# A hybrid encoder trunk: Fourier weight tiles by output half, q swaps right behind the eviction, exponentials scaled on GpSimd

## The chip, the cores and the metric

The kernel runs on one core of one Trainium2 chip. The metric is the device time of one execution in microseconds. Before the change the median of three runs is 2400.9 us (2396.56 to 2402.89).

## What is computed

Two layers over 272 tokens (16 meta tokens and 256 real ones), model width 2048, all in float32. Per layer, cut to what matters here:

```
h = rmsnorm(x);  [q | k | v | f | ga | gf] = h @ w_in
attention: 8 query heads on 2 key heads of 128; q and k are normalised
           per head and rotated (rope on four quarters of 32 channels)
           p = softmax(q k^T / sqrt(128));  o = p v
fourier:   Re(2-D DFT over positions and the 128 channels of a group) of f
a = o @ w_attn_br;  s = fourier @ w_four
x = x + (sigmoid(ga) * a + sigmoid(gf) * s) @ w_out
x = x + w_down( silu(dwconv3(rmsnorm(x) @ w_up_gate)) * (rmsnorm(x) @ w_up_val) )
```

## The kernel before, in words

Activations lie transposed in SBUF, channels on partitions. Each weight passes through once as a stream of chunks of 512 KB: 128 partitions by 4 blocks of 256 columns. SyncE's queue loads a chunk into one of seven `raw` buffers (`load_raw`). For precision each float32 operand is split in two parts: ScalarE casts the high part `wh` (line 300), VectorE subtracts for the low part `wl` (line 303), each with three buffers. A matmul group then takes three products per block, high by high, high by low and low by high (lines 372 to 374).

The order of the work is the order in which the program emits it. `order` lists all weight groups. `advance(upto)` issues loads up to seven chunks past `upto` and puts the splits up to `upto` on a list; `pump()` emits one of that list after every second triple of matmuls, and `pump(i)` emits all up to chunk i. Side work (norm statistics, rotation, attention, the DFT) sits in generators on a `shadow` list; `step()` advances one of them at each of the same points, and a yielded number is how many steps that generator rests. A scheduler then lays the instructions into the queues of the engines. Two things bind it: instructions under `keep_in_program_order` stay where they were emitted, and inside `manual_schedule(engines=...)` so does all work of the named engines.

Three places are touched.

**The Fourier branch, `four_group`.** Each of the eight groups per layer computes s for 256 outputs in two halves m of 128. Its 8 row blocks of w_four come as two chunks. A chunk holds half the input rows of both output halves, so each half m runs through both chunks (loop j, then c, then the even and odd part e): sixteen matmuls per half on lines 407 (high weights on high and low data at once) and 408 (low weights), and one matmul for the remaining channels (line 413). `pump(i0 + 1)` emits both chunks' splits ahead of the first matmul. In layer 0 each of these chunks is first folded on VectorE (`fold_w`, line 291: sums and differences of row halves) into the tile `wpm`, which has one buffer; the split reads `wpm`. Layer 1's chunks were folded earlier and stored (`prefold`).

**q.** After each of the four q groups per layer, `head_evac` (lines 910 and 911) reads the product from PSUM: squares into `qps` on ScalarE, the scaled q into `qp` on VectorE. Then the generator `q_stage` is pushed. Its first step issues `swap` (line 924): four DMAs from SyncE's queue that write qp with neighbouring quarters of 32 partitions exchanged into `qs`. Later steps take the statistics (lines 918 to 1029, the power of line 513 on GpSimd) and rotate: `rope` (lines 928 to 933) multiplies qs by the sines and qp by the cosines, adds and splits. The tiles qp, qps and qs share seven buffers (tag "r") with the gates and with layer 1's folding. In layer 1 q group 1 and the folded Fourier projection behind it (`folded_f`, 16 chunks of folded weights `fw`, matmuls of lines 843 to 847) run with VectorE's order written by hand; so the rotation of q0 stands at a fixed place in VectorE's queue, between splits.

**Attention.** Per key head there are nine items of 128 query rows: one of meta tokens and eight of a head and a block. `scores` makes the product into PSUM, its row maximum and the exponentials `pe` with their sum `sm` (line 1078). `normalise` takes the reciprocal `rs` (line 1083) and multiplies pe by it into `pn`, in two VectorE instructions (lines 1086 and 1087; the second writes the 16 meta columns three times). An iteration later `transposed` turns pn on TensorE (line 1095) and splits it into PH and PL (lines 1108, 1109); after another iteration `values` multiplies by v (lines 1118 to 1121). Matmuls of the q and gate groups run between the steps. GpSimd has little to do in this stage; its queue carries the DMAs that add up weights for the last layer (`weight_sums`, lines 558 and 559), each behind a one-column copy `tick` from the newest low part.

Of the kernel before, what the change touches and what calls it, by code (L numbers as in the profile page):

```python
# [13 lines left out]
ALU = mybir.AluOpType  # L14
AX = mybir.AxisListType

P = 128
D = 2048
NM = 16
SEQ = 256  # L20
T = NM + SEQ
# [5 lines left out]
NG = 8  # L27
# [5 lines left out]
CW = 4  # L33
MG = 2
# [43 lines left out]
TH = T // 2 + 2  # L78
# [75 lines left out]
def _rep(ap, n):  # L154
    return ap.unsqueeze(1).to_broadcast([ap.shape[0], n, ap.shape[1]])
# [8 lines left out]
def st2(ap):  # L164
    if len(ap.shape) == 3:
        return ap.rearrange("p r (a b) -> p r a b", b=2)
    return ap.rearrange("p (a b) -> p a b", b=2)
# [11 lines left out]
def encoder_kernel(ctx, tc, xT, params, consts, bmat, cfold, csign, w_fl, w_f64c, w_in, w_abr, w_four, w_f64, w_out, w_up, w_down, w_vn, w_dn, w_dt, out):  # L179
    nc = tc.nc  # L180
# [12 lines left out]
    for l in range(DEPTH):  # L193
# [13 lines left out]
        for half in range(2):  # L207
            for kind, j in BRANCH_ORDER[half]:
                w, off, n = {"ga": (w_in, IN_GA, KT), "gf": (w_in, IN_GF, KT), "s": (w_four, 0, 8), "a": (w_abr, 0, 8)}[kind]
# [25 lines left out]
    t, done = 0, 0  # L235
    for key, chs in order:
        for j, ch in enumerate(chs):
            n = 0
            if key[0] == 1 and key[1] in ("t", "ug", "uv"):
                n = due(t) - done  # L240
# [40 lines left out]
    def pump(upto=None):  # L281
        if upto is None:
            if todo:
                todo.pop(0)[1]()
        while upto is not None and todo and todo[0][0] <= upto:
            todo.pop(0)[1]()
# [101 lines left out]
    def four_group(key, fr, x64, w64, evac):  # L388
        k, chs = order[st["grp"]]
        assert k == key, (k, key)  # L390
        st["grp"] += 1
        i0 = st["next"]
        st["next"] += len(chs)
        advance(i0 + 1 + LOOK)
        pump(i0 + 1)
        ws = [splits.pop(i0 + j) for j in range(2)]
        for m in range(MG):
            sl = slice(m * P, (m + 1) * P)
            ps = [psum.tile([P, 512], F32, tag="mm", name=f"ps_s{m}{e}") for e in range(2)]
            for j in range(2):  # L400
                h, lo = ws[j]
                for c in range(2):
                    kt = 2 * j + c
                    for e in range(2):
                        x = al(fr[:, kt, e])
                        o2 = st2(ps[e][:, :2 * TH].rearrange("p (r n) -> p r n", r=2))
                        nc.tensor.matmul(o2, h[:, 2 * e + c, sl], x, start=kt == 0, stop=False)
                        nc.tensor.matmul(st2(ps[e][:, :TH]), lo[:, 2 * e + c, sl], x[:, 0], start=False, stop=e == 1 and kt == 3)
                    step()
                    pump()  # L410
                if m == 1 and j == 0:
                    advance(i0 + 2 + LOOK)
            nc.tensor.matmul(st2(ps[0][:, :TH]), w64[:, sl], al(x64), start=False, stop=True)
            evac(m, ps)
# [194 lines left out]
    for l in range(DEPTH):  # L609
# [6 lines left out]
        with tc.tile_pool(name=f"mix{l}", bufs=1) as mp:  # L616
# [285 lines left out]
            def head_evac(ps, gcol, name, lo):  # L902
                hp = rt(name)
                sq = rt(name + "s")
                if lo:
                    nc.gpsimd.memset(hp[:, :, 0:lo], 0.0)
                    nc.gpsimd.memset(sq[:, :, 0:lo], 0.0)
                for m in range(MG):
                    x = de(ps[m][:, :T - lo])
                    nc.scalar.activation(hv(sq[:, m, lo:T]), x, AF.Square)  # L910
                    nc.vector.scalar_tensor_tensor(hv(hp[:, m, lo:T]), x, gcol, hv(rstdB[:, lo:T]), op0=ALU.mult, op1=ALU.mult)
                return hp, sq
# [8 lines left out]
            def swap(hp):  # L921
                qs = rt("qs")
                for b in range(4):
                    tc.keep_in_program_order(nc.sync.dma_start(qs[32 * b:32 * b + 32, :, :], hp[32 * (b ^ 1):32 * (b ^ 1) + 32, :, :]))
                return qs
# [82 lines left out]
            for pn in pns:  # L1008
                nc.gpsimd.memset(pn[:, 0:P], 0.0)

            def q_stage(i, qp, qsq):
                kv, j = i // 2, i % 2
                sl = slice(2 * j, 2 * j + 2)
                if j == 0:
                    qvs.append(small.tile([P, 9], F32, tag="qv", name="qv"))
                    qsms.append(small.tile([P, 2, 4, NM], F32, tag="sqm", name="sqm", bufs=2))
                qv, qsm = qvs[kv], qsms[kv]
                qs = swap(qp)
                yield 3
                nc.vector.tensor_copy(qsm[:, :, 2 * j:2 * j + 2, :], qsq[:, :, 0:NM].unsqueeze(1).to_broadcast([P, 2, 2, NM]))  # L1020
                d4 = qv[:, 4 * j:4 * j + 4]
                sums_t(d4, [qsq[:, m, a:b] for m in range(MG) for a, b in BLK[1:]])
                d4 = d4.rearrange("p (m i) -> p m i", m=2)
                nc.vector.tensor_tensor(d4, d4, bc2(tok2[:, 1:3]), op=ALU.mult)
                if j:
                    yield 1
                    sums_t(qv[:, 8:9], [qsm.rearrange("p r h t -> p (r h t)")])
                    nc.vector.tensor_tensor(qv[:, 8:9], qv[:, 8:9], tok2[:, 0:1], op=ALU.mult)
                    nc.vector.tensor_scalar(qv, qv, 1.0 / HD, EPS, op0=ALU.mult, op1=ALU.add)
                    rq = small.tile([P, 9], F32, tag="rq", name="rq")  # L1030
                    pow_half(rq, qv)
                yield 6 - j
                yield from rope(qp, qs, qH[kv][:, sl, :], qL[kv][:, sl, :])
                if j:
                    rqs.append(rq)
                    if kv == 0:
                        push(attend(), 5)
# [9 lines left out]
            def attention(kv, rq):  # L1047
# [33 lines left out]
                def normalise(pe, sm):  # L1081
                    rs = small.tile([P, 1], F32, tag="rs", name="rs")
                    nc.vector.reciprocal(rs, sm)
                    pn = pns[cnt[0] % 3]
                    cnt[0] += 1
                    nc.vector.tensor_scalar(pn[:, P:3 * P], pe[:, NM:T], rs, None, op0=ALU.mult)
                    nc.vector.tensor_scalar(pn[:, 0:96].rearrange("p (a b) -> p a b", b=32)[:, :, 0:NM], _rep(pe[:, 0:NM], 3),
                                            rs, None, op0=ALU.mult)
                    return pn

# [60 lines left out]
            for i in range(4):  # L1151
                if not (last and i == 1):
                    ps = group((l, "q", i), xr(lo), W)
                    qq = head_evac(ps, prm[:, P_QN + l:P_QN + l + 1], "qp", lo)
                if last:
                    if i in (0, 2):
                        until(hold, "vt" if i == 0 else "fold")
                        for t_, n in ((qH, "q1"), (qL, "q2")):
                            t_.append(mp.tile([P, 4, T], F32R, tag=n + "ab"[i // 2], name=n))
                elif i == 0:  # L1160
                    until(hold, "vt")
                    until(hold, "fold")
                    for t_, n in ((qH, "q1"), (qL, "q2")):
                        t = mp.tile([P, NH, T], F32R, tag=n, name=n)
                        t_ += [t[:, 0:4], t[:, 4:8]]
                if last and i == 1:
                    until(hold, "ahead")
                    with tc.manual_schedule(engines={mybir.EngineType.DVE}):
                        ps = group((l, "q", i), xr(lo), W)
                        with tc.manual_schedule(engines={mybir.EngineType.Activation}):  # L1170
                            qq = head_evac(ps, prm[:, P_QN + l:P_QN + l + 1], "qp", lo)
                            folded_f(slots, E)
                    o1_tiles()
                    push(folded_chan(E), 1)
                push(q_stage(i, *qq), 1)
# [327 lines left out]
def _tiles(w):  # L1503
    d, k, m = w.shape
    return np.ascontiguousarray(
        w.reshape(d, k // (CW * P), CW, P, m // (MG * P), MG * P).transpose(0, 4, 1, 3, 2, 5)
    )


def _four(w):  # L1510
    d = w.shape[0]
    wz = np.concatenate([w, np.zeros((d, 1, D), w.dtype)], 1)
    c = np.arange(HC)
    pair = lambda q: [np.concatenate([P * g + c for g in (2 * q, 2 * q + 1)]),
                      np.concatenate([np.where(c == 0, NG * P, P * g + P - c) for g in (2 * q, 2 * q + 1)])]
    rows = np.concatenate([pair(2 * h + q)[k] for h in range(2) for k in range(2) for q in range(2)])
    w64 = np.zeros((d, 64, D), w.dtype)
    w64[:, 0:8] = w64[:, 32:40] = w[:, [P * (2 * i + m) + HC for m in range(2) for i in range(4)]]
    w64 = np.ascontiguousarray(w64.reshape(d, 64, NG, MG * P).transpose(0, 2, 1, 3))
    return _tiles(wz[:, rows]), w64  # L1520


def _fl(w):
# [47 lines left out]
```

## Time and profile before

| | us |
|---|---|
| median of 3 runs | 2400.9 |
| the profiled execution | 2399.24 |
| its span, first to last instruction | 2397.2 |
| TensorE busy | 2367.0 (99%) |
| VectorE busy | 1819.8 (76%) |
| ScalarE busy | 1307.1 (55%) |
| GpSimd busy | 133.4 (6%) |

The span and the busy times come from one profiled execution. Its stages, in us from the span's start:

| stretch | what runs | TensorE busy | VectorE busy |
|---|---|---|---|
| 0 to 85 | layer 0: norm, f, k, v | 80.00 | 64.59 |
| 85 to 470 | layer 0: q, attention, gates, Fourier and attention branches, first half of w_out | 375.94 | 297.49 |
| 470 to 1240 | layer 0: rest of w_out, feed-forward | 770.00 | 523.84 |
| 1240 to 1680 | layer 1: k to the branches, first half of w_out | 430.42 | 336.15 |
| 1680 to 2397 | layer 1: rest of w_out, feed-forward | 710.62 | 597.77 |

How to read the rows below: a row of a group names the line, engine, operation and tensors (out<-in), the count, and after the bar busy time and mean ns of one. A row of the timeline has start and length in us, and in brackets how long the engine sat idle before and what ended that. A row of the waits names who waited for whom: total us, times, longest. A row of stretches gives the length, each engine's busy us with its instructions in brackets, then the granted clock of TensorE as a share, the DMA share and GB/s. PE is TensorE, PEld its weight loads, DVE VectorE, ACT ScalarE, POOL GpSimd, SPq SyncE's queue. Matmuls are pipelined, so one of 272 columns spans 0.28 us though the next starts 0.116 us after it.

### The profile page before, as it was taken

What the parts mean: (1) busy time and instruction counts of PE and PEld (TensorE: products, weight loads), DVE (VectorE), ACT (ScalarE), POOL (GpSimd) and SP (SyncE); (2) the same over time, 40 slices, a digit from 0 to 9 for tenths busy, and PEclk for the clock granted to TensorE, in tenths of its full rate; (3) what the DMA queues carried; (4) which work ended last, traced back from release to release, by engine and by line L of the source; (5) the groups of instructions that cost most, each with busy time, mean ns of one, the idle gap of its engine ahead of it and who ended that gap; (6) DMA issues with size and microseconds to landing.
All of it is one profiled execution on the core that took longest, in us unless ns stands there. A gap on an engine that the chain in (4) does not pass through costs nothing.

```text
span 2397.2 us, 47622 instructions
## 1 busy us (share of the span) xinstructions
PE 2367.0 (99%) x18992; PEld 2305.8 (96%) x18992; DVE 1819.8 (76%) x2889; ACT 1307.1 (55%) x1893; POOL 133.4 (6%) x265
## 2 busy tenths in 40 slices
PE   9999999999999999999999999999999999999999
PEld 8999999999999999999998999999989999999988
DVE  7787867877767556777568887776878889888798
ACT  6555534554444334444455555445676666666565
POOL 0000100100000000000000000000000000000000
PEclk9999999999999999999999999999999999999999
DMA  7556999989999999999875646888889988988887
GB/s 278 173 159 216 289 295 304 297 278 346 313 303 327 315 330 314 316 327 308 264 256 181 190 150 216 264 291 247 290 294 301 323 291 301 305 304 279 260 279 251
DMA packets 171215, 660.69 MB, mean 276 GB/s; under 512 B 19424, under 2 KB 24672, under 8 KB 170096
## 3 DMA queue, kind: packets, MB, share of 16 engines
q1 hardware_dynamic: 152528, 538.07, 64.0%
q0 software_dynamic: 17024, 117.45, 19.4%
q8 instruction: 149, 2.44, 0.4%
q10 hardware_dynamic: 1440, 2.13, 0.3%
q14 instruction: 74, 0.61, 0.1%
HBM read 635.91 MB, written 136.31 MB: 322 GB/s over the span
## 4 chain that ended last, share of the span: by engine, by line
PE 81%; DVE 6%; ACT 2%; DMA 1%; issue 1%; SPq 0%; POOL 0%; ACTq 0%; DVEq 0%; POOLq 0%
PE ps_p L1415 9%; PE ps_ug L374 6%; PE ps_ug L373 6%; PE ps_ug L372 6%; PE ps_uv L368 4%; PE ps_d L374 3%; PE ps_uv L373 3%; PE ps_uv L372 3%; PE ps_d L373 3%; PE ps_uv L374 3%; PE ps_d L372 3%; DVE wl L303 3%; PE ps_o L372 2%; PE ps_o L373 2%; PE ps_o L374 2%; PE ps_uv L369 2%
## 5 line engine op out<-in xcount | busy, mean ns | idle before, releaser
L303 DVE TENSOR_TENSOR wl<-raw,wh 128x1024 fp32r<-128x1024 f32 (+1 forms) x937 | 1127.6, 1217 | 469.8 <-ACT wh L300 458.4
L300 ACT CAST wh<-raw 128x1024 fp32r<-128x1024 f32 (+1 forms) x937 | 964.6, 1040 | 752.1 <-PE ps_ug L373 197.2
L374 PE MATMUL ps_ug<-xHL,wl 128*128 128x272 f32 (+1 forms) x1408 | 390.6, 277 | 0.8 <-DVE wl L303 0.6
L372 PE MATMUL ps_ug<-xHL,wh 128*128 128x272 f32 (+1 forms) x1408 | 390.7, 278 | 0.0
L373 PE MATMUL ps_ug<-xHL,wh 128*128 128x272 f32 (+1 forms) x1408 | 390.0, 277 | 0.0
L373 PEld LDWEIGHTS ps_ug<-xHL,wh 128*128 128x128 f32 x1408 | 267.4, 190 | 2.1
L372 PEld LDWEIGHTS ps_ug<-xHL,wh 128*128 128x128 f32 x1408 | 267.4, 190 | 2.1
L374 PEld LDWEIGHTS ps_ug<-xHL,wl 128*128 128x128 f32 x1408 | 267.5, 190 | 1.6 <-DVE wl L303 1.5
L372 PE MATMUL ps_uv<-xHL,wh 128*128 128x272 f32 x704 | 196.4, 279 | 0.0
L373 PE MATMUL ps_uv<-xHL,wh 128*128 128x272 f32 x704 | 196.4, 279 | 0.0
L374 PE MATMUL ps_uv<-xHL,wl 128*128 128x272 f32 x704 | 196.4, 279 | 0.0
L372 PE MATMUL ps_d<-gHL,wh 128*128 128x272 f32 x704 | 196.4, 279 | 0.0
L373 PE MATMUL ps_d<-gHL,wh 128*128 128x272 f32 x704 | 196.4, 279 | 0.0
L374 PE MATMUL ps_d<-gHL,wl 128*128 128x272 f32 x704 | 196.4, 279 | 0.0
L1415 PE MATMUL ps_p<-wh,opnd 128*128 128x512 f32 x688 | 177.5, 380 | 0.5 <-ACT wh L300 0.5
L368 PE MATMUL ps_uv<-xHL,wh 128*128 128x512 f32 x448 | 150.8, 383 | 0.1
L372 PE MATMUL ps_ga<-xHL,wh 128*128 128x272 f32 (+1 forms) x512 | 144.0, 281 | 0.0
L372 PE MATMUL ps_gf<-xHL,wh 128*128 128x272 f32 (+1 forms) x512 | 143.0, 279 | 0.0
L374 PE MATMUL ps_gf<-xHL,wl 128*128 128x272 f32 (+1 forms) x512 | 141.8, 277 | 0.0
L373 PE MATMUL ps_ga<-xHL,wh 128*128 128x272 f32 (+1 forms) x512 | 141.8, 277 | 0.0
L374 PE MATMUL ps_ga<-xHL,wl 128*128 128x272 f32 (+1 forms) x512 | 141.8, 277 | 0.0
L373 PE MATMUL ps_gf<-xHL,wh 128*128 128x272 f32 (+1 forms) x512 | 141.8, 277 | 0.0
(372 smaller groups left out, 5840.8 us busy)
## 6 DMA issues: line engine op xcount, KB each, us to landing
raw<-in_w_up SPq DMA_DIRECT2D x320, 512.0 KB, 5.6
raw<-in_w_in SPq DMA_DIRECT2D x191, 512.0 KB, 4.5
raw<-in_w_down SPq DMA_DIRECT2D x88, 512.0 KB, 6.8
raw<-ft SPq DMA_DIRECT2D x80, 512.0 KB, 4.8
raw<-in_w_out SPq DMA_DIRECT2D x64, 512.0 KB, 6.5
ft<-in_w_dn POOLq DMA_DIRECT2D x30, 1024.0 KB, 12.1
raw<-in_w_dn SPq DMA_DIRECT2D x60, 512.0 KB, 5.0
raw<-in_w_abr SPq DMA_DIRECT2D x32, 512.0 KB, 5.6
```

The source lines that it names most:

```text
L300: nc.scalar.copy(h[:, a:b], r[:, a:b])
L303: nc.vector.tensor_tensor(lo[:, a:b], r[:, a:b], h[:, a:b].bitcast(F32), op=ALU.subtract)
L368: nc.tensor.matmul(o2, h[:, c, sl], ab, start=kt == 0, stop=False)
L369: nc.tensor.matmul(o, lo[:, c, sl], ab[:, 0], start=False, stop=kt == nk - 1)
L372: nc.tensor.matmul(o, h[:, c, sl], a, start=kt == 0, stop=False)
L373: nc.tensor.matmul(o, h[:, c, sl], b, start=False, stop=False)
L374: nc.tensor.matmul(o, lo[:, c, sl], a, start=False, stop=kt == nk - 1)
L1415: nc.tensor.matmul(st2(ps[h]), x, al(w[:, 512 * h:512 * h + 512]), start=fresh and (s_, q) in BEGIN and first, stop=(s_, q) in END and end ...
```

## The change

Three edits, and the host's layout of one weight:

- `w_four` is laid out anew, so that a chunk holds all input rows of 128 outputs, instead of half the rows of 256. Each half m of a Fourier group takes one chunk whole. The splits of chunk i0 + m are forced just ahead of half m, and the next `advance` comes at the end of half 0 instead of after the first chunk of half 1. The fold adds and subtracts the same halves of a chunk as before.
- `swap` of q is called right behind `head_evac`, ahead of everything of the next group, and its tile is handed to `q_stage`. The swap of k stays where it was.
- The two multiplications of `normalise` are issued on GpSimd.

```
@@ four_group
         advance(i0 + 1 + LOOK)
-        pump(i0 + 1)
-        ws = [splits.pop(i0 + j) for j in range(2)]
         for m in range(MG):
             sl = slice(m * P, (m + 1) * P)
             ps = [psum.tile([P, 512], F32, tag="mm", name=f"ps_s{m}{e}") for e in range(2)]
+            pump(i0 + m)
+            h, lo = (w.rearrange("p c n -> p (c n)").rearrange("p (e k n) -> p e k n", e=2, k=4) for w in splits.pop(i0 + m))
             for j in range(2):
-                h, lo = ws[j]
                 for c in range(2):
                     kt = 2 * j + c
...
-                        nc.tensor.matmul(o2, h[:, 2 * e + c, sl], x, start=kt == 0, stop=False)
-                        nc.tensor.matmul(st2(ps[e][:, :TH]), lo[:, 2 * e + c, sl], x[:, 0], start=False, stop=e == 1 and kt == 3)
+                        nc.tensor.matmul(o2, h[:, e, kt], x, start=kt == 0, stop=False)
+                        nc.tensor.matmul(st2(ps[e][:, :TH]), lo[:, e, kt], x[:, 0], start=False, stop=e == 1 and kt == 3)
                     step()
                     pump()
-                if m == 1 and j == 0:
+                if m == 0 and j == 1:
                     advance(i0 + 2 + LOOK)
@@ q_stage
-            def q_stage(i, qp, qsq):
+            def q_stage(i, qp, qsq, qs):
...
-                qs = swap(qp)
                 yield 3
@@ normalise
-                    nc.vector.tensor_scalar(pn[:, P:3 * P], pe[:, NM:T], rs, None, op0=ALU.mult)
-                    nc.vector.tensor_scalar(pn[:, 0:96].rearrange("p (a b) -> p a b", b=32)[:, :, 0:NM], _rep(pe[:, 0:NM], 3),
+                    nc.gpsimd.tensor_scalar(pn[:, P:3 * P], pe[:, NM:T], rs, None, op0=ALU.mult)
+                    nc.gpsimd.tensor_scalar(pn[:, 0:96].rearrange("p (a b) -> p a b", b=32)[:, :, 0:NM], _rep(pe[:, 0:NM], 3),
                                             rs, None, op0=ALU.mult)
@@ the q groups (both places)
                     qq = head_evac(ps, prm[:, P_QN + l:P_QN + l + 1], "qp", lo)
+                    qq += (swap(qq[0]),)
@@ _four (host)
-    return _tiles(wz[:, rows]), w64
+    t = _tiles(wz[:, rows]).reshape(d, NG, 2, P, 2, 2, MG, P).transpose(0, 1, 6, 3, 4, 2, 5, 7)
+    return np.ascontiguousarray(t).reshape(d, NG, MG, P, CW, MG * P), w64
```

More of the change, by code (lines that the diff above doesn't have):

```diff
@@ L1171, in encoder_kernel @@
                             qq = head_evac(ps, prm[:, P_QN + l:P_QN + l + 1], "qp", lo)
+                            qq += (swap(qq[0]),)
                             folded_f(slots, E)
```

## The prediction

> **What bounds the kernel now.** I read the page's first part, then the waits of the matmul engine, then the stretches in which those waits lie.
>
> ```profile
> span 2397.2 us, 47622 instructions
> ## 1 busy us (share of the span) xinstructions
> PE 2367.0 (99%) x18992; PEld 2305.8 (96%) x18992; DVE 1819.8 (76%) x2889; ACT 1307.1 (55%) x1893; POOL 133.4 (6%) x265
> ```
>
> PE is busy 99% of the span, and the change removes no matmul. Only PE's own holes can be won back: 30.2 us of plain idle time, and what a lower clock or a modelled end hides inside "busy". PE's waits between 120 and 1700 us, longest first (total us, times, longest):
>
> ```profile
> PE ps_s L408 <- DVE wl L303: 4.3, 8, 0.7
> PE ps_f L847 <- DVE wl L303: 3.9, 1, 3.9
> PE ps_pt L1095 <- DVE pn L1086: 2.9, 4, 1.3
> PE ps_pv L1119 <- DVE PL L1109: 2.2, 4, 1.2
> PE ps_pv L1118 <- ACT PH L1108: 2.0, 5, 0.5
> PE ps_s L407 <- ACT wh L300: 2.0, 5, 1.1
> ```
>
> First and last row: the Fourier groups (ps_s) wait for the split of a weight tile, 6.3 us. Second row: one single wait of 3.9 us in the folded projection of layer 1. The other three, 7.1 us, are attention's. Each of these is the place of one edit.
>
> **Edit 1, the Fourier tile.** A group is 34 matmuls on two tiles. Five of layer 0's eight groups, each from its first matmul to the next group's, and last one of layer 1 (the first number after the stretch is its length):
>
> ```profile
> 222.67:228.74 6.07, 4.34 (x34) 3.99 (x34) 0.51 (x2) 0.45 (x2) 1.00 0.33 99
> 245.47:250.71 5.24, 4.34 (x34) 3.98 (x34) 0.50 (x2) 0.44 (x2) 1.00 0.91 222
> 355.73:360.98 5.25, 4.34 (x34) 3.99 (x34) 0.51 (x2) 0.45 (x2) 1.00 0.93 311
> 388.83:393.31 4.48, 4.12 (x34) 3.92 (x34) 0.51 (x2) 0.45 (x2) 1.00 0.65 164
> 453.50:457.99 4.49, 4.13 (x34) 3.93 (x34) 0.51 (x2) 0.45 (x2) 1.00 0.71 276
> 1576.37:1580.22 3.85, 3.85 (x34) 3.85 (x34) 0.50 (x2) 0.45 (x2) 1.00 0.60 193
> ```
>
> The same 34 matmuls take 3.85 us when nothing is late. Layer 0 loses 2.22 us in its first group, about 1.4 in each of four (the second and third rows are the first and last of them), about 0.63 in each of three (the fourth and fifth rows): 2.22 + 4 x 1.4 + 3 x 0.63 = 9.7 us. Inside another of the four, which began at 289.35, and VectorE's (DVE) load beside it:
>
> ```profile
> 290.58 0.62 PE L407 MATMUL ps_s<-fr,wh 128*128 128x276 f32 x3 [0.20 <-ACT wh L300]
> 291.84 0.44 PE L408 MATMUL ps_s<-fr,wl 128*128 128x138 f32 x2 [0.64 <-DVE wl L303]
> ```
> ```profile
> 289.40:294.50 5.10, 4.26 (x35) 3.91 (x35) 5.01 (x11) 3.91 (x7) 0.00 (x0) 1.00 0.83 339
> ```
>
> The second tile is asked for a quarter of the way in, and both its halves are late: in layer 0 a tile is folded before it is split, through one wpm buffer, so two tiles come one after the other. After the change output half m=0 needs tile 0 alone, and tile 1 is asked for after half the group instead of a quarter, 3.85/4 = 0.96 us later. Each group keeps what exceeds that: 1.26, four times 0.44, three times nothing, 3.0 in all; 6.7 us are won. Matmuls, shapes, loads and splits stay as many. Tile 0's buffers come free at half instead of three quarters and the next `advance` moves up as far, at no cost, since both only let loads and splits start sooner. But VectorE works 5.01 of 5.10 us there, so PE, arriving earlier at the next group, will sometimes find the next tile unfinished. I take a fifth back, 1.3 us (bounds: nothing, and 0.44 in each of eight groups, 3.5). **Edit 1: -5.4 us** (-3.2 to -6.7).
>
> **Edit 2, the q swaps.** The second wait, with the tensors of VectorE and SyncE (SPq) that lead to it:
>
> ```profile
> 1293.55 0.29 PE L846 MATMUL ps_f<-hA,w64s 128*16 128x138 f32 x2
> 1297.73 0.48 PE L847 MATMUL ps_f<-hA,wl 128*128 128x138 f32 x1 [3.89 <-DVE wl L303]
> ```
> ```profile
> 1284.32 0.48 DVE L911 SCALAR_TENSOR_TENSOR qp<-ps_q,prm,rstdB 128x258 f32<-128x258 f32 x1
> ...
> 1292.93 0.73 DVE L928 TENSOR_TENSOR qs<-qs,cst 128x544 f32<-128x544 f32 x1 [2.54 <-DMA qs<-qp]
> ...
> 1296.45 1.22 DVE L303 TENSOR_TENSOR wl<-raw,wh 128x1024 fp32r<-128x1024 f32 x1
> ```
> ```profile
> 1282.65 4.30 SPq L264 DMA_DIRECT2D raw<-fw  x2
> 1287.05 2.52 SPq L924 DMA_DIRECT2D qs<-qp  x4
> ```
>
> In this stage VectorE's order is written by hand, and the rotation of q (L928) stands ahead of the split of the second folded tile. VectorE sits idle 2.54 us until the swap has landed, and PE 3.89 us for the split behind it. The swap waited for nothing of its own: qp was ready at 1284.32 + 0.48 = 1284.80, but a weight load of the next group stood ahead of it in SyncE's queue until a raw buffer came free. Emitted at once after the eviction, the four swaps stand ahead of that load: they issue at 1284.85 instead of 1287.05 and land 2.2 us sooner. VectorE, free from 1292.93 - 2.54 = 1290.39, starts L928 at 1290.73, all behind it moves up by 2.2, and PE's hole shrinks from 3.89 to 1.7 us. That is not all:
>
> ```profile
> 1297.70:1303.60 5.90, 5.87 (x27) 5.79 (x28) 3.14 (x5) 1.99 (x2) 0.00 (x0) 0.50 0.52 178
> 1303.60:1327.00 23.40, 23.40 (x210) 23.13 (x210) 22.86 (x32) 16.38 (x24) 0.12 (x1) 1.00 0.79 256
> ```
> ```profile
> 162.44 0.52 PE L1095 MATMUL ps_pt<-cst,pn 128*128 128x128 f32 x3 [1.26 <-DVE pn L1086]
> ```
> ```profile
> 123.00:215.30 92.30, 89.63 (x769) 88.68 (x769) 76.15 (x188) 51.16 (x108) 4.29 (x5) 1.00 0.52 172
> ```
>
> After the hole the granted clock is 0.50 for 5.9 us: work of 2.95 us. The hole of 1.26 us at 162.44 cost no clock (1.00 over 123 to 215). The remaining 1.7 us is far nearer to that than to 3.89, so I count the 2.9 us as won. The Trainium skill (TensorE: Matmul & The Clock Gate, Part 1) puts the idle time that halves the clock at about 3.4 us; by it, too, 1.7 us keeps the full clock, and no run here shows a hole between 1.26 and 3.89.
>
> Taken back: VectorE is busy 22.86 of the next 23.40 us, so PE at full clock runs into its splits; 0.5 us (0 to 2). The swap of q1 now stands ahead of the folded tiles' loads and holds SyncE until q1 is evicted (two evictions of 0.48 us behind the late split) and for 2.52 us of issue: about 3.5 us on the loads behind it. What hides them is that a load is issued seven raw buffers ahead of its split; without that lead the 3.5 us would show in full. The other swaps end no PE wait above: nothing. The qs tiles are now taken with qp and qps, from the same seven buffers; two sets of three are alive at a time, and with w64s in the folded stage that makes seven. **Edit 2: -2.2 - 2.9 + 0.5 = -4.6 us** (-5.6 to 0).
>
> **Edit 3, the exponentials.** VectorE loses 36 pairs:
>
> ```profile
> L1086 DVE TENSOR_SCALAR pn<-pe,rs x36: 343/353/355, 127.8 to 1451.8; 128x256 f32<-128x256 f32 x36
> L1087 DVE TENSOR_SCALAR pn<-pe,rs x36: 243/246/268, 128.0 to 1452.1; 128x48 f32<-128x48 f32 x36
> ```
>
> 36 x (0.353 + 0.246) = 21.6 us off VectorE, which is busy 76.15 of 92.30 us in layer 0's attention. GpSimd (POOL) gets them, plus a hand-over after the reciprocal. No row shows it multiplying; the nearest:
>
> ```profile
> L493 POOL MEMSET V<- 128x256 f32 x1 | 0.3, 315 | 0.0
> ```
> ```profile
> L513 POOL TENSOR_TENSOR rq<-qv,mhalf 128x9 f32<-128x9 f32 x4 | 8.2, 2043 | 107.9 <-DVE qv L1029 107.9
> ```
>
> A memset of the same 256 columns takes 0.315 us; a power costs 2.043/9 = 0.227 us per column. Below, 304 columns at the memset's price are 304 x 0.315/256 = 0.4 us; above, at the power's price, 304 x 0.227 = 69 us. I take 0.85 us with two starts and the hand-over, near the memset, the one row of this width, and 0.25 more than VectorE's pair; the upper end is left to the third rival. What hides it:
>
> ```profile
> 186.21 0.25 DVE L1087 TENSOR_SCALAR pn<-pe,rs 128x48 f32<-128x48 f32 x1
> ```
> ```profile
> 188.22 0.38 PE L1095 MATMUL ps_pt<-cst,pn 128*128 128x128 f32 x2
> ```
>
> In this item pn is ready at 186.46 and the transposes start at 188.22: 1.76 us of cover. Only 4 of 36 items have none (the third wait row); those pay 4 x 0.25 = 1.0 us. Behind a waiting pn on GpSimd stand its later pairs, the weight-sum DMAs and the next rq power, none due sooner. In return the 4.2 us of waits for PL and PH shrink, as far as VectorE's queue makes them: its idle share in the stretch rises from 17% to 29% (10.8 us less in each layer). I take a quarter of them, 1.0 us. **Edit 3: 0** (-4, all of those waits, to +6, the second rival).
>
> **Sum.** -5.4 - 4.6 + 0 = -10.0 us. The profiled execution took 2399.24 us (span 2397.2 and 2.0 around it), 1.7 below the median 2400.9 of runs from 2396.56 to 2402.89. So 2389.2 for it, and 2390.9, say 2391.0, as a median. A measurement can tell about 0.3%, 7.2 us.
>
> **The rivals.**
> - *The swap stays where it was.* If the compiled SyncE queue still holds the load ahead of the swap, or the swap's landing is not what ends last, edit 2 gives nothing: -5.4, 2395.5 us. For: both the load and the swap become ready within 2.2 us, and the order is settled before the kernel runs, from estimates. Against: the swap is pinned to program order (`keep_in_program_order`). Chance 0.18.
> - *GpSimd and VectorE block each other.* Here a one-column copy, beside two splits:
>
> ```profile
> 296.69 1.05 POOL L558 COPY tick<-wl 128x1 f32<-128x1 f32 x1 [12.42 <-DVE wl L303]
> ```
> ```profile
> 295.34 2.35 DVE L303 TENSOR_TENSOR wl<-raw,wh 128x1024 fp32r<-128x1024 f32 x2
> ```
>
> It lasts until 297.74, the splits until 297.69: GpSimd was held for the second split, 1.22 us. If pn meets a split each time, the four items without cover pay 1.22 + 0.25 = 1.5 us each, 6 us, and VectorE wins nothing: -10.0 + 6 = -4, 2397 us. Against: after the reciprocal VectorE often has work on PSUM next. Chance 0.14. The Trainium skill (SBUF — State Buffer, Who interferes with whom) states this as an exclusive lock between a VectorE instruction with two SBUF inputs and a GpSimd one that reads SBUF; the copy above agrees.
> - *Slower: GpSimd is the bound of attention.* From 0.60 + 1.76 = 2.4 us per pair on, even an item with typical cover makes PE wait. At 10 ns per column, a twentieth of the power's price, a pair is 3.1 us, 0.7 too late in each of 36 items: +25 - 10 = +15, 2416 us. Over 2.9 us per pair the gain is lost by more than 0.3%. Against: the memset's 1.2 ns per column. Chance 0.06.
>
> **How the numbers follow.** My forecast has 0.58; what is left, 0.04, is a mixture around no change. Faster by over 0.3% (below 2393.7) is the forecast: 0.58. Within 0.3% are the first two rivals and most of the rest: 0.35. Slower: 0.07. Range: below, edits 1 and 2 at their better bounds (nothing taken back, and half a us from a swap that lands sooner still) and half of attention's, -6.7 - 5.6 - 2 = -14.3, 2386.5; above, both first rivals together, -5.4 + 6 = +0.6, 2401.5.
>
> **What would show it.** Right: Fourier groups of layer 0 near 3.9 to 4.3 us, the first near 5; four swaps before 1287 in terms of the old trace, VectorE's wait for qs under 0.5 us, PE's hole near 1.7 us and a granted clock of 1.00 after it; 72 GpSimd multiplies, a pair under 1 us, and waits of ps_pt near 3 us. Wrong: ps_s still waiting over 4 us, a clock of 0.50 near 1300, or ps_pt <- POOL pn over 10 us.

## The result, and the profile after

The changed kernel takes 2404.38 us (median of 16 runs, 2401.84 to 2406.05); the kernel before, beside it, 2400.79 (16 runs, 2396.56 to 2403.67). The ratio is 1.0017, 95% interval 1.0009 to 1.0024: slower by 3.6 us, where 10 us of gain were forecast, and above the upper end of the range. The profiled execution's span is 2401.4 us. The page's first part of the changed kernel:

```profile
span 2401.4 us, 47653 instructions
...
PE 2366.2 (99%) x18992; PEld 2302.5 (96%) x18992; DVE 1804.0 (75%) x2817; ACT 1306.8 (54%) x1893; POOL 192.6 (8%) x337
```

VectorE's busy time fell by 15.8 us (by 21.0 as a sum of durations, since neighbouring rows overlap), GpSimd's rose by 59.2. PE's waits between 120 and 1700 us, the view in which the prediction found its three places:

```profile
PE ps_gf L372 <- DVE se L1207: 5.3, 6, 1.6
PE ps_a L372 <- DVE se L1207: 5.2, 8, 0.9
PE ps_ga L372 <- DVE se L1207: 2.1, 2, 1.6
PE ps_pt L1093 <- POOL pn L1084: 2.0, 3, 1.0
PE ps_pt L1093 <- POOL pn L1085: 1.8, 3, 0.7
PE ps_pv L1116 <- ACT PH L1106: 1.5, 3, 0.6
PE ps_f L846 <- DVE wl L303: 1.4, 2, 1.3
PE ps_s L407 <- DVE wl L303: 1.2, 4, 0.3
```

The waits inside the Fourier groups fell as meant, from 6.3 us to 1.2 (last row). The folded projection's wait fell from 3.9 to 1.4. But the first three rows are new: 12.6 us in 16 waits, one for each Fourier group. What waits is the first matmul of the group *behind* it, for the eviction of the Fourier accumulators (`s_evac`): ScalarE copies one part of each of a half's two accumulators to SBUF (`se`, `so`), and VectorE adds the other part to the copy. Only then is the PSUM bank free. Two stretches of the changed kernel, each from a Fourier group's first matmul to that of the next group, one of layer 0 and one of layer 1:

```profile
288.86:295.00 6.14, 4.29 (x37) 3.94 (x35) 6.09 (x12) 4.97 (x8) 0.13 (x1) 1.00 0.61 235
1575.65:1580.15 4.50, 4.02 (x36) 3.88 (x35) 3.25 (x6) 3.06 (x5) 0.13 (x1) 1.00 0.66 198
```

In layer 1, where nothing was late before (3.86 us), 4.50. The three engines at the end of that last group, first PE, then ScalarE and VectorE:

```profile
1577.44 0.27 PE L412 MATMUL ps_s<-x,w 96*128 96x138 f32 x1
1579.39 0.27 PE L412 MATMUL ps_s<-x,w 96*128 96x138 f32 x1
1580.15 0.38 PE L372 MATMUL ps_a<-q,wh 128*128 128x258 f32 x1 [0.48 <-DVE se L1207]
```
```profile
1577.58 1.05 ACT L300 CAST wh<-raw 128x1024 fp32r<-128x1024 f32 x1 [0.80 <-PE ps_s L406]
1578.53 0.27 ACT L1206 COPY se<-ps_s 128x138 f32<-128x138 f32 x1
1578.70 0.28 ACT L1206 COPY so<-ps_s 128x138 f32<-128x138 f32 x1
```
```profile
1578.66 1.23 DVE L303 TENSOR_TENSOR wl<-raw,wh 128x1024 fp32r<-128x1024 f32 x1 [0.62 <-ACT wh L300]
1579.80 0.30 DVE L1207 TENSOR_TENSOR se<-ps_s,se 128x138 f32<-128x138 f32 x1
1580.01 0.29 DVE L1207 TENSOR_TENSOR so<-ps_s,so 128x138 f32<-128x138 f32 x1
```

Half 0's last matmul is the first PE row, ending at 1577.71. Its eviction should follow. Instead ScalarE starts a split at 1577.58: it had waited for a *matmul of half 0* (the bracket), because that matmul is the last reader of chunk i0's `wh` buffer, which is free from there on. The small matmul of line 412 comes after it, so the buffer is free a moment before the accumulators are complete. The split takes 1.05 us on ScalarE and 1.23 on VectorE, both ahead of the eviction. The next group wants the two banks of half 0, as the matmul groups share four. The first of them is free at 1579.80 + 0.30 = 1580.10, and the group starts at 1580.15. The same place in the kernel before, ScalarE and VectorE:

```profile
1578.36 0.28 ACT L1206 COPY so<-ps_s 128x138 f32<-128x138 f32 x1 [0.86 <-PE ps_s L408]
1578.53 0.28 ACT L1206 COPY se<-ps_s 128x138 f32<-128x138 f32 x1
1579.33 1.99 ACT L300 CAST wh<-raw 128x1024 fp32r<-128x1024 f32 x2 [0.52 <-PE ps_s L407]
```
```profile
1578.67 0.29 DVE L1207 TENSOR_TENSOR so<-ps_s,so 128x138 f32<-128x138 f32 x1
1578.88 0.29 DVE L1207 TENSOR_TENSOR se<-ps_s,se 128x138 f32<-128x138 f32 x1
```

There the chunk's buffer came free at three quarters of the group, after the eviction of half 0 had ended at 1579.17, a full microsecond before the group's end.

The second edit is in the changed kernel as forecast. q's eviction and its swap on SyncE's queue, then PE's two waits and the stretch around them:

```profile
1286.08 0.48 DVE L910 SCALAR_TENSOR_TENSOR qp<-ps_q,prm,rstdB 128x258 f32<-128x258 f32 x1
```
```profile
1286.63 2.52 SPq L923 DMA_DIRECT2D qs<-qp  x4
```
```profile
1296.86 0.33 PE L846 MATMUL ps_f<-hA,wl 128*128 128x138 f32 x1 [1.26 <-DVE wl L303]
1303.78 0.33 PE L846 MATMUL ps_f<-hA,wl 128*128 128x138 f32 x1 [0.18 <-DVE wl L303]
```
```profile
1290.00:1304.00 14.00, 12.56 (x111) 12.04 (x111) 12.10 (x17) 6.69 (x11) 0.00 (x0) 1.00 0.71 231
```

The swap issues 0.07 us behind the eviction, the hole is 1.26 us in place of 3.89, and the granted clock stays at 1.00. Between the starts of the Fourier projection and of the q groups behind it, the changed kernel gains 4.95 us on the kernel before.

The third edit: the two multiplies on GpSimd (min, median and max ns), one pair beside a split on VectorE, and VectorE's load in layer 0's attention.

```profile
L1084 POOL TENSOR_SCALAR pn<-pe,rs x36: 913/924/1821, 126.8 to 1448.6; 128x256 f32<-128x256 f32 x36
```
```profile
L1085 POOL TENSOR_SCALAR pn<-pe,rs x36: 392/405/1437, 127.7 to 1449.5; 128x48 f32<-128x48 f32 x36
```
```profile
128.29 0.92 POOL L1084 TENSOR_SCALAR pn<-pe,rs 128x256 f32<-128x256 f32 x1 [0.22 <-DVE rs L1081]
129.19 1.28 POOL L1085 TENSOR_SCALAR pn<-pe,rs 128x48 f32<-128x48 f32 x1
```
```profile
128.97 1.23 DVE L303 TENSOR_TENSOR wl<-raw,wh 128x1024 fp32r<-128x1024 f32 x1 [0.77 <-ACT wh L300]
```
```profile
120.00:212.00 92.00, 90.27 (x775) 89.05 (x774) 70.36 (x155) 53.21 (x111) 35.31 (x40) 1.00 0.53 176
```

By the medians a pair takes 924 + 405 = 1329 ns, not 850. The multiply at 129.19 took 1.28 us instead of 0.41: a split had begun before it, and it ended at 130.47, 0.27 us after that split (128.97 + 1.23 = 130.20). The split took its usual 1.23. Of the 72 multiplies of the trace 16 are longer than usual, 15 of them behind a split that had begun before; so the mean of a pair is 1.71 us.

### The profile page after: what moved, and what is told of

Same layout as the page of the kernel before. It is cut to its first block, busy times and chain, and to the rows that moved or that the text cites. A ratio compares the mean times of both kernels' runs of the same rounds, so it can differ in the third digit from the quotient of the medians.

```text
span 2401.4 us, 47653 instructions
## 1 busy us (share of the span) xinstructions
PE 2366.2 (99%) x18992; PEld 2302.5 (96%) x18992; DVE 1804.0 (75%) x2817; ACT 1306.8 (54%) x1893; POOL 192.6 (8%) x337
## 4 chain that ended last, share of the span: by engine, by line
PE 86%; DVE 7%; ACT 2%; DMA 2%; issue 2%; POOL 1%; SPq 0%; DVEq 0%; ACTq 0%; POOLq 0%
PE ps_p L1415 9%; PE ps_ug L374 6%; PE ps_ug L373 6%; PE ps_ug L372 6%; DVE wl L303 4%; PE ps_uv L368 4%; PE ps_d L373 3%; PE ps_uv L372 3%; PE ps_uv L374 3%; PE ps_d L372 3%; PE ps_uv L373 3%; PE ps_d L374 3%; PE ps_o L374 2%; PE ps_o L373 2%; PE ps_o L372 2%; PE ps_gf L372 2%
## 5 line engine op out<-in xcount | busy, mean ns | idle before, releaser
L557 POOL COPY tick<-wl 128x1 f32<-128x1 f32 x112 | 32.9, 294 | 1524.1 <-DVE wl L303 1524.1
```

The source lines that it names most:

```text
L557: tc.keep_in_program_order(nc.gpsimd.tensor_copy(tick, st["wl"][:, 0, 0:1].bitcast(F32)))
```

## The experiments

**Theory A**: the new tile lets chunk i0 go just as half 0's eviction becomes ready; the split of a later chunk gets ahead of the eviction, and the next group waits for its PSUM banks. The rivals are named in each expectation. All times are medians; the ratio is to the kernel before beside it. The group lengths are read from the timelines, from a Fourier group's first matmul to the next group's (layer 1 without its first, which has attention inside).

| kernel | us | ratio (95%) | layer 0, eight groups, us | layer 1, us |
|---|---|---|---|---|
| before | 2400.79 | | 6.07 5.24 5.18 5.18 5.25 4.48 4.49 4.48 | 3.86 |
| changed | 2404.38 | 1.0017 (1.0009 to 1.0024) | 5.23 6.19 6.12 6.14 5.04 4.88 4.93 4.88 | 4.50 to 4.62 |
| 1: old tile | 2393.45 | 0.9969 (0.9960 to 0.9978) | 4.98 5.25 5.18 5.25 5.25 4.49 4.49 4.48 | 3.86 |
| 2: q swaps alone | 2397.02 | 0.9983 (0.9974 to 0.9992) | 6.06 5.24 5.18 5.18 5.25 4.48 4.49 4.48 | 3.86 |
| 3: other banks | 2388.28 | 0.9949 (0.9934 to 0.9965) | 4.19 4.45 4.38 4.45 4.45 3.85 3.85 3.85 | 3.86 |
| 4: request put back | 2404.06 | 1.0012 (1.0002 to 1.0021) | 5.23 6.19 6.12 6.14 5.04 4.87 4.93 4.88 | 4.50 to 4.61 |
| 5: order pinned | 2400.54 | 0.9998 (0.9989 to 1.0007) | 4.28 6.13 6.07 6.13 4.45 4.88 4.87 4.93 | 4.26 to 4.32 (3), 3.86 (4) |
| 6: old tile, other banks | 2394.86 | 0.9971 (0.9961 to 0.9981) | 4.98 5.24 5.18 5.25 5.24 4.48 4.48 4.48 | 3.86 |
| 7: other banks, pn on VectorE | 2391.12 | 0.9956 (0.9944 to 0.9969) | 5.27 4.45 4.38 4.38 4.45 3.85 3.86 3.85 | 3.86 |
| 8: new tile alone | 2412.00 | 1.0044 (1.0029 to 1.0060) | 6.31 6.19 6.12 6.07 5.05 4.88 4.93 4.88 | 4.50 to 4.62 |
| 9: other banks, order pinned | 2395.27 | 0.9982 (0.9973 to 0.9991) | 4.19 4.67 4.59 4.60 4.45 3.86 3.86 3.85 | 3.86 |
| 10: other banks, wide multiply twice | 2396.51 | 0.9991 (0.9982 to 1.0000) | as 3 | 3.86 |

### 1 and 2: which edit loses

Experiment 1 puts `four_group` and the host's layout back and keeps the other two edits; experiment 2 also puts `pn` back on VectorE.

```diff
-            pump(i0 + m)
-            h, lo = (w.rearrange("p c n -> p (c n)").rearrange("p (e k n) -> p e k n", e=2, k=4) for w in splits.pop(i0 + m))
+        pump(i0 + 1)
+        ws = [splits.pop(i0 + j) for j in range(2)]
...
-                if m == 0 and j == 1:
+                if m == 1 and j == 0:
```

> The Fourier groups are put back as before (tile and loop), the q swaps and the GpSimd multiplies stay. Theory A (the new Fourier tile costs what the rest wins: its first tile comes free just as the first half's eviction becomes ready, so the split of a later tile gets ahead of that eviction in ScalarE's and VectorE's queues, and the next group waits for its PSUM banks): the waits of ps_gf, ps_ga and ps_a for se (12.6 us in 16 in the changed kernel) are gone, the groups of layer 1 are 3.86 us instead of 4.6, those of layer 0 as before, and the time is about 5 us below the kernel before, 2394 to 2397. Rival B (GpSimd's multiplies cost it, not the tile): no better than the changed kernel, 2402 to 2406. Rival C (the q swaps give their gain back later): about 2400, as the kernel before.

> The q swaps alone are moved; Fourier tile and the multiplies as before. Theory A: one hole of 1.4 us instead of 3.9 in the folded projection of layer 1, granted clock 1.00 behind it, about 5 us below the kernel before, 2394 to 2397. Its difference to the run with swaps and GpSimd multiplies is what GpSimd does: theory A says within 2 us either way (about 1 us for GpSimd); rival B (GpSimd's multiplies cost it) says that this one is 4 us or more the faster of the two. Rival C: about 2400.

Without the new tile the kernel is 10.9 us faster than the changed one (11.5 by the ratios) and 0.31% faster than the kernel before, at 2393.45 half a microsecond under theory A's span. Every wait for se is gone, the groups of layer 1 are at 3.86. Added over all sixteen groups the new tile costs 9.4 of these 10.9 us. Rivals B and C fall. The q swaps alone give 0.17%, at the slow end of theory A's span. The GpSimd multiplies gain 3.6 us between these two kernels, more than theory A's "within 2 us" and with the sign against rival B. In the timelines 0.8 us of it come in layer 0's attention and 1.1 in the first Fourier group behind it (6.06 against 4.98).

### 3: other banks

```diff
-            ps = [psum.tile([P, 512], F32, tag="mm", name=f"ps_s{m}{e}") for e in range(2)]
+            ps = [psum.tile([P, 512], F32, tag="aux" if m else "mm", name=f"ps_s{m}{e}") for e in range(2)]
```

> The changed kernel, with the second half's two PSUM accumulators of a Fourier group taken from the other pair of banks, so that the next group's banks no longer hang on the eviction of the first half. Theory A: the order in ScalarE's and VectorE's queues stays and the first half's eviction is as late, but the waits for se in front of ps_gf, ps_ga and ps_a go from 12.6 us to under 2; layer 1's groups are back at 3.86 us instead of 4.6 and layer 0's below those of the kernel before, mostly 4 to 5; 2389 to 2394. Rival D (VectorE's work itself is what the groups wait for, whatever the banks): the wait only moves to the matmul behind, groups of layer 1 stay at 4.5 us, 2401 to 2405.

The time is 2388.28 us, a little under theory A's span and the fastest of the study: below the kernel before by 0.51% and below the changed one by 16 us. No wait for se is left. One group of each layer, and VectorE at the end of the second:

```profile
283.89:288.35 4.46, 4.13 (x37) 3.93 (x35) 4.41 (x9) 3.52 (x5) 0.00 (x0) 1.00 0.73 297
...
1562.68:1566.54 3.86, 3.86 (x37) 3.86 (x35) 2.60 (x4) 2.44 (x4) 0.00 (x0) 1.00 0.70 222
```
```profile
1565.69 1.23 DVE L303 TENSOR_TENSOR wl<-raw,wh 128x1024 fp32r<-128x1024 f32 x1 [0.62 <-ACT wh L300]
1566.83 0.30 DVE L1207 TENSOR_TENSOR se<-ps_s,se 128x138 f32<-128x138 f32 x1
```

The split still stands ahead of the eviction. The eviction starts at 1566.83, 0.29 us after the next group, and costs nothing, as that group now takes banks that were free long before. So it is the banks through which the late eviction reached PE. Rival D falls.

### 4: the request put back

```diff
-                if m == 0 and j == 1:
+                if m == 1 and j == 0:
```

> The changed kernel, with the request for further tiles in a Fourier group put back from the half to the three-quarter point. Rival E (it is this request, moved forward, that puts a split ahead of the first half's eviction): the waits for se go, layer 1's groups are at 3.86 us, and the time falls by 8 us or more, to 2392 to 2396. Theory A (the split is ready as soon as the first tile is let go, wherever it was requested): the waits for se stay near 12 us, the groups of layer 1 at 4.5 us, 2402 to 2406.

The same waits to a tenth (5.3, 5.2 and 2.1 us), the same groups, the same time. Where `advance` stands is not the cause; rival E falls.

### 5 and 9: the order pinned

Experiment 5 keeps the changed kernel's banks and pins the eviction's copies and additions, and the splits emitted inside `four_group`, to program order. Experiment 9 does this and has the other banks too.

```diff
-                                nc.scalar.copy(hv(a), de(p_[:, TH:2 * TH]))
-                                nc.vector.tensor_tensor(hv(a), de(p_[:, :TH]), hv(a), op=ALU.add)
+                                tc.keep_in_program_order(nc.scalar.copy(hv(a), de(p_[:, TH:2 * TH])))
+                                tc.keep_in_program_order(nc.vector.tensor_tensor(hv(a), de(p_[:, :TH]), hv(a), op=ALU.add))
...
+            keep = tc.keep_in_program_order if st.get("pin") else (lambda v: v)
-            nc.scalar.copy(h[:, a:b], r[:, a:b])
+            keep(nc.scalar.copy(h[:, a:b], r[:, a:b]))
...
+        st["pin"] = True
         for m in range(MG):
...
+        st["pin"] = False
```

> The changed kernel with the same PSUM banks, but the copies and additions that empty a Fourier half, and the splits asked for inside a Fourier group, are pinned to program order, so that in ScalarE's and VectorE's queues the eviction of the first half stands ahead of the split that overtook it. Theory A: what costs is that split ahead of the eviction, so the banks come free in time and the waits for se go from 12.6 us to under 3; layer 1's groups are at 3.86 to 3.95 us, layer 0's at 4 to 5; 2389 to 2395. Rival F (the first half's eviction is too late for the next group whatever stands ahead of it: 0.62 us copies and two additions after the last matmul of the half): waits for se of 5 us or more remain, layer 1's groups stay over 4.2, 2397 to 2403.

> The changed kernel with both remedies: the second half's accumulators from the other pair of banks, and evictions and splits of a Fourier group pinned to program order. With the other banks alone the groups took 4.19, 4.38 to 4.45 and 3.85 us in layer 0 and 3.86 in layer 1; with the pinned order alone 4.28, 6.07 to 6.13 and 4.45 to 4.93, and 3.86 to 4.32. Theory A (the banks are what the next group waits for, the order only what makes them late): with the banks untied the order gains nothing more; the groups stay as with the banks alone, 2387 to 2390. Rival I (the late eviction costs something beside the banks): 1 us or more below the kernel with the banks alone, under 2387.

Experiment 5 is mostly rival F's: 8.0 us of waits for se remain, and it won 3.8 of the 10.9 us of loss. One group of layer 0 and two of layer 1 in its trace, and ScalarE in the first of them:

```profile
288.17:294.30 6.13, 4.29 (x37) 3.95 (x35) 5.04 (x11) 4.32 (x8) 0.00 (x0) 1.00 0.64 261
1469.22:1473.48 4.26, 4.02 (x36) 3.88 (x34) 3.54 (x9) 3.28 (x7) 1.00 (x2) 1.00 0.76 188
1573.55:1577.40 3.85, 3.85 (x36) 3.85 (x35) 3.13 (x9) 2.44 (x4) 0.00 (x0) 1.00 0.79 269
```
```profile
291.35 0.42 ACT L1232 CAST mH<-th 128x272 fp32r<-128x272 f32 x1 [1.68 <-DVE th L1231]
291.67 1.04 ACT L301 CAST wh<-raw 128x1024 fp32r<-128x1024 f32 x1
292.62 0.27 ACT L1210 COPY se<-ps_s 128x138 f32<-128x138 f32 x1
```

In the last four groups of layer 1 the overtaking split was all there was, and they are at 3.86, as theory A has it. The first and the fifth group of layer 0, at 4.28 and 4.45, and the first of layer 1 are mended too. Six groups of layer 0 stay as long as in the changed kernel, and three of layer 1 are mended in part. In the group of the ScalarE rows two other things stand ahead of the eviction, and both come before it in program order: the end of the eviction of the `a` group, which waits for VectorE, and another split. So half 0, whose last matmul ends at 290.23, is not copied before 292.62. An overtaking split is thus the whole cause in seven of the sixteen groups; behind the nine others PE still waits for se. And the pin has a price. Experiment 9 is 7 us slower than experiment 3, where theory A had expected no change and rival I a gain; two of the waits in its trace that experiment 3 does not have:

```profile
PE ps_gf L376 <- DVE wl L305: 1.6, 2, 0.8
...
PE ps_a L376 <- DVE wl L305: 1.1, 3, 0.4
```

Splits held behind an eviction are late for the next group: PE waits for them 0.4 to 0.8 us in six places of layer 0. With the banks untied, the scheduler's order, split first, was the better of the two that were run.

### 6: the banks alone

Experiment 1 with the edit of experiment 3.

> A control: the old Fourier tile and loop with the q swaps and the GpSimd multiplies, and the second half's accumulators from the other pair of banks. It tells whether the other banks are a gain in themselves. Theory A: the old groups waited for splits, not for banks, so layer 0's groups stay at 4.98 to 5.25 and 4.49 us, layer 1's at 3.86, and the time is that of the same kernel without the other banks, 2393.5, within 1.5 us. Rival G (the other banks gain by themselves, the new tile nothing): about 2388, as the changed kernel with those banks.

Within 1.5 us of experiment 1 in time, and in each group within 0.02. With the old tile nothing waits for banks; rival G falls.

### 7: GpSimd's part, once more

> The changed kernel with the second half's accumulators from the other pair of banks, and the scaling of the exponentials back on VectorE. It prices the GpSimd multiplies a second time, now with the new tile. The first time it was 3.6 us by the medians (2397.0 without, 2393.5 with them) and 3.2 us by the traces, of which 0.8 us came in layer 0's attention, 1.1 us in the first Fourier group (5.0 us against 6.1), 1.0 us in the projections behind layer 1's Fourier stage. If that is the multiplies' doing, this kernel is 2 to 4 us slower than with them: 2390 to 2392.5, with the first Fourier group of layer 0 about 5 us against 4.19. If it was chance between runs, 2387.5 to 2389.5.

2391.12 against 2388.28: 2.8 us (1.7 by the ratios, whose intervals overlap), inside the span expected if it is the multiplies' doing. The timelines show the same two steps as between experiments 1 and 2, 0.8 us in layer 0's attention and 1.1 in the first group (5.27 against 4.19). The third, in layer 1's projections, is not there: 1.0 us of the first difference stays unexplained.

### 8: the new tile alone

> The new Fourier tile alone; swaps and multiplies as before. Theory A: its loss is its own and doesn't depend on the other two: waits for se of about 12 us, layer 1's groups at 4.5 to 4.6 us, 8 to 11 us above the kernel before, 2409 to 2413. Rival H (the tile loses only beside the other two, through what they do to the queues): near the kernel before or below, 2395 to 2403.

2412.0 us, 0.44% above the kernel before and inside theory A's span; rival H falls. The tile's loss is its own: the groups cost the same 9.4 us. A part on top of it is new, the granted clock. The 4 us after each of its four longest holes of these stages (the clock is the third figure from the end), and PE's rows at the first two:

```profile
252.25:256.25 4.00, 4.00 (x20) 4.00 (x21) 3.84 (x11) 0.74 (x3) 0.69 (x2) 0.57 1.03 316
276.81:280.81 4.00, 4.00 (x34) 4.00 (x35) 3.84 (x11) 1.73 (x4) 1.07 (x2) 1.00 1.03 316
299.67:303.67 4.00, 4.00 (x20) 4.00 (x21) 3.84 (x11) 0.74 (x3) 0.56 (x2) 0.57 1.27 476
1304.24:1308.24 4.00, 4.00 (x18) 4.00 (x19) 1.86 (x3) 0.45 (x1) 0.00 (x0) 0.50 0.62 229
```
```profile
252.25 0.60 PE L372 MATMUL ps_gf<-xHL,wh 128*128 128x272 f32 x1 [1.58 <-DVE se L1206]
...
276.81 0.38 PE L372 MATMUL ps_ga<-xHL,wh 128*128 128x272 f32 x1 [1.58 <-DVE se L1206]
```

The holes at 252.25 and 276.81 are equally long. Behind the first PE does 20 matmuls in 4 us, behind the second 34. Each of the two stretches at 0.57 loses 4 x 0.43 = 1.7 us of work. The fourth hole is the one near 1300 that the kernel before has too, here 2.29 us instead of 3.89. The sum, 9.4 + 2 x 1.7 - 1.6 = 11.2 us, is the measured loss.

### 10: the edge of the GpSimd cover

Experiment 3 with the wide multiply issued twice, so that a pair takes 2.25 us.

```diff
-                    nc.gpsimd.tensor_scalar(pn[:, P:3 * P], pe[:, NM:T], rs, None, op0=ALU.mult)
+                    for _ in range(2):
+                        nc.gpsimd.tensor_scalar(pn[:, P:3 * P], pe[:, NM:T], rs, None, op0=ALU.mult)
```

> The changed kernel with the other pair of banks, and GpSimd's wide multiply of each item issued twice (the second repeats the first, the values are the same), so that a pair takes about 0.92 + 0.92 + 0.40 = 2.24 us instead of 1.33. It looks for the edge that the prediction put at 2.4 us per pair (0.60 of VectorE's pair and 1.76 us of cover of a typical item). If the edge is right, only items with less than typical cover pay: up to 0.9 us in each of the 6 items that already make TensorE wait and less in others, 3 to 8 us, 2391 to 2397. If GpSimd is the bound of attention from there on, 0.9 us in each of 36 items: 30 us, 2418 or more. If GpSimd has cover to spare everywhere: no change, 2387 to 2390.

8.2 us slower than experiment 3 (10 by the ratios), at the upper end of the 3 to 8 us expected if the edge is right. PE's waits for pn in this trace, and the longest:

```profile
PE ps_pt L1094 <- POOL pn L1085: 11.4, 11, 2.2
```
```profile
1363.51 0.55 PE L1094 MATMUL ps_pt<-cst,pn 128*128 128x128 f32 x3 [2.21 <-POOL pn L1085]
```

11 of the 36 items wait, in place of 6; 0.92 us more in each of 36 would have been 33 us. The edge is near: at 1.33 us (the median) a pair is covered in 30 of 36 items, at 2.25 in 25.

## Why the prediction was wrong, point by point

**Edit 1 is the step that failed.** The prediction wrote that tile 0's buffers come free at half instead of three quarters "at no cost, since both only let loads and splits start sooner". A split that starts sooner takes 1.05 us of ScalarE and 1.23 us of VectorE sooner, and what was queued behind it was the eviction of the banks that the next group needs. The prediction named who waits on PE for the tile, but not who waits in those two queues behind the split. In place of -5.4 us the tile measured +10.9 (changed kernel against experiment 1). The second thing in that sentence, the `advance` moved forward, did cost nothing (experiment 4). The rest of the working stands: with the banks untied the tile is worth 2393.45 - 2388.28 = 5.2 us (6.6 against experiment 6), near the 5.4, and layer 0's groups keep 0.34, four times about 0.58 and nothing in three, 2.7 us. Forecast were 3.0 for the late second tile and 1.3 taken back. The 0.34 of the first group is edit 3's doing in part: without it the group keeps 1.42 (experiment 7), near the 1.26 of the working. The group still waits for wl, 1.2 us in four waits.

**Edit 2 was right.** Forecast -4.6; 4.95 us at its place, 4.1 by the ratio of experiment 2 (1.9 to 6.2). The swap issued at once, VectorE did not wait for qs, the hole was 1.26 us and the clock 1.00. The step from a hole of 1.7 us to a full clock was not safe, though: in experiment 8 holes of 1.52 and 1.58 us lost it. That the hole came out shorter than forecast, at 1.26, was luck.

**Edit 3 was mis-sized in both terms.** The pair takes 1.33 us by the medians and 1.71 by the mean, not 0.85; ps_pt waits 3.8 us in 6 for GpSimd, forecast about 3. VectorE's relief was worth more than the one quarter of attention's waits: those for PL and PH fell from 4.2 to 2.0 us, and the first Fourier group, which the sum had not looked at, gained 1.1 us. That VectorE comes out of attention with less behind it is the likely reason; no run tests it. Together the edit gives -3.6 and -2.8 us in the two pairs of kernels (-3.4 and -1.7 by the ratios); forecast was 0.

**The rivals.** None of them is what happened. The swap did move. GpSimd is held by a split, as the second rival had it, in 15 of the 72 multiplies and not each time, and VectorE won all the same. GpSimd is not the bound at 1.33 us a pair; it becomes one in part at 2.25. The slower side had been given to GpSimd, 0.07; it came from the edit that I had the firmest numbers for.

## What to carry to other kernels

A buffer that comes free earlier isn't free of cost: look up what then becomes ready, on which in-order queues it runs, and which eviction stands behind it there. Before accumulators are emptied more often or at another point, count the banks and ask which later group wants the same ones. If the order in the queues can't be made right for all, untie the dependence (other banks) rather than pin the order.

## What the runs showed of the hardware

- **The clock after a hole doesn't follow from its length.** Holes up to 1.27 us never cost clock in these traces. Of those of 1.50 to 2.21 us, most cost none (three in the changed kernel of 1.52 to 1.58 us, three in experiment 5, and in experiment 10 one of 2.21 us, clock 1.00 after it), but in experiment 8 one of 1.58 and one of 1.52 halved it for the next stretch, and 2.29 and 3.89 did too. The Trainium skill (TensorE: Matmul & The Clock Gate, Part 1) has the clock halved after an idle window of about 3.4 us that runs freely. The measurement differs: 1.52 and 1.58 us were enough. It agrees in that the clock changes on a fixed grid: in experiment 8 it rises at 13.32, is halved from 252.25 to 255.66 and from 300.04 to 303.45, and again from 1303.56 to 1310.38, all whole multiples of 3.413 us apart. But where a hole falls on that grid doesn't decide alone. Experiment 8's holes of 1.58 and 1.52 us that halved the clock each lie inside one step of the grid; so does the changed kernel's first of 1.58 us (247.59 to 249.17, counted from its clock's rise at 8.18), and it cost nothing. What else decides stays open.
- **A GpSimd multiply by a column of scalars** costs, by the medians of the two shapes here, (924 - 405) / (256 - 48) = 2.5 ns per column and about 0.29 us besides; the memset from which I estimated took 1.2 ns per column. VectorE's same pair took 0.60 us.
- **A GpSimd multiply is held by a VectorE split** that began before it: 1.28 us in place of 0.41 in the rows above, and 15 such cases in the trace. The Trainium skill (SBUF — State Buffer, Who interferes with whom) has it as a lock between a VectorE instruction with two SBUF inputs and a GpSimd one that reads SBUF; the trace agrees. The other way round no holding shows: the splits that began inside a multiply kept 1.22 to 1.26 us.
